# Reordered first loads and first squares, and a final norm's root taken with tokens on partitions, in a 2-layer decoder step on one core

## The chip, the cores and the metric

The kernel runs on one core of a Trainium2 chip, in one launch. The metric is the time of one execution on the device in microseconds (us), as the median of three runs. A profiled execution gives the trace from which the rows below are taken; its own time stands beside its span.

## What is computed

320 tokens (256 of a prompt, 64 of eight samples) of 1024 channels go through two layers, each a half-step SwiGLU, a mixer with three branches, and a second half-step SwiGLU, with an RMSNorm ahead of each and one at the end:

```python
def rmsnorm(x, g):
    y = xf * lax.rsqrt(jnp.mean(xf * xf, axis=-1, keepdims=True) + EPS)
    return y * g
for l in range(DEPTH):                       # DEPTH = 2
    x = x + 0.5 * swiglu_ffn(rmsnorm(x, ffn1_norm), w_gu, w_down)
    h = rmsnorm(x, mix_norm);  [u | v | q | g] = h @ w_in
    x = x + merged(pool(u), conv(v), attention(q), g) @ w_out
    x = x + 0.5 * swiglu_ffn(rmsnorm(x, ffn2_norm), w_gu2, w_down2)
y = rmsnorm(x, final_norm)
```

The change touches the very first RMSNorm and the loads ahead of it, the last RMSNorm, and the place at which a small state of the pooling branch is loaded.

## The kernel before

**Layout.** Channels lie on the 128 partitions: `x` is 128 x 8 x 320, eight blocks of 128 channels with the 320 tokens along the free dimension. A channel mean is therefore a matmul with a 128x128 matrix `ones` of value 1/1024, whose result stands on all partitions.

**Matmuls.** A product in full precision is made of three matmuls of split operands: the weight's high part times the activation's high and low parts (lines 306 and 307), then the weight's low part times the activation's high part (line 309). `chain` does this for 8 blocks at a time: 16 matmuls with `whi`, then 8 with `wlo`. These 24 matmuls use one half (128x1024) of a 1 MB weight tile `raw`; such a half is called a **unit** here and counted from 1.

**Weights.** `Stream` loads `raw` tiles through the queue of SyncE (SP), four in flight (`NRAW`), and `split` makes `whi` on ScalarE (ACT, a cast) and `wlo` on VectorE (DVE, a subtraction). There are four buffers each (`NW`), so the split of unit 9 writes the buffers of unit 5 and has to wait until TensorE (PE) has read them.

**The first SwiGLU.** The activations `hhi`, `hlo` are `x` times the norm's gain, split (`split_scaled`: ACT, then DVE, line 358 for ACT). They are not yet divided by the root of the mean square; that factor, `rstd`, is multiplied in when a result leaves PSUM (`sg<-mm,rstd`, `up<-mm,rstd`), since it depends only on the token. Products of units 1, 2, 3, 4, 5 go to PSUM buffers mm, mm, mm, cv, cv (`pwide`; three mm and two cv); unit 6 takes the mm buffer of unit 1 again, which is free when `sg<-mm,rstd` of unit 1 has read it.

**The factor.** `rsqrt_ops` is a chain of ten dependent DVE operations (`rx`) on 128x320, the last of which writes `rstd`. Ahead of it `first_mean` squares the eight blocks of `x` on GpSimd (POOL) and adds them up with eight matmuls on `ones` (line 901).

**The end.** The last mean is two matmuls on `ones` (lines 948 and 949: the sum of seven blocks' squares, and the eighth's square `last`), then `rsqrt_now` on 128x320, then `x` times `rstd`: blocks 6 and 7 on POOL, blocks 0 to 5 on DVE in three operations of 128x640, and the stores.

**Order.** The order of each engine's instructions is made when the program is built, by a scheduler that moves them; the order that came out is shown with the change. Operations on DVE and POOL are issued through a helper and all have line 124.

Of the kernel before, what the change touches and what calls it, by code (L numbers as in the profile page):

```python
# [15 lines left out]
P = 128  # L16
# [68 lines left out]
def trunk_kernel(  # L85
# [67 lines left out]
    def pst():  # L153
        return psum("st", 2)
# [3 lines left out]
    nc.scalar.dma_start(cst[:, :8], c_in[:, :8])  # L158
# [14 lines left out]
    class Stream:  # L173
# [11 lines left out]
        def issue(self):  # L185
            while self.pos < len(items) and self.live < NRAW:
# [10 lines left out]
                if it == ("w", 0):  # L197
                    for i in range(4):
                        if i < 2:
                            nc.sync.dma_start(t[:, 512 * i:512 * i + 512], src[:, 512 * i:512 * i + 512])  # L200
                        nc.sync.dma_start(x[:, 2 * i:2 * i + 2, :], x_in[:, 2 * i:2 * i + 2, :])
                    nc.sync.dma_start(t[:, 1024:], src[:, 1024:])
                    nc.gpsimd.dma_start(cst[:, 8:], c_in[:, 8:])
                else:
                    nc.sync.dma_start(t[:, :], src)
# [216 lines left out]
    def deferred_norm(l, off, squares=True):  # L422
# [4 lines left out]
        def on_block(o):  # L427
            split_scaled(x[:, o, :], ccol(l, off, o), h[0][:, o, :], h[1][:, o, :])
            if squares:
                st.add(x[:, o, :])  # L430
# [252 lines left out]
    def mixer(l, mh, acc, on_block):  # L683
# [81 lines left out]
        for g in range(4):  # L765
            ut = tp.tile([P, 2, UW], F32, name=nm("ut"), tag="ut", bufs=2)
            pool.memset(ut[:, :, 0:PB], 0.0)
            nc.gpsimd.dma_start(ut[:, :, PB + T:UW], sp_in[l, :, 2 * g:2 * g + 2, :])
# [120 lines left out]
    h, st, on_block = deferred_norm(0, C_G1, squares=False)  # L889
    for o in range(KB):  # L890
        if o % 4 == 1:
            ws.split(ws.nsplit)
            ws.nsplit += 1
        on_block(o)

    def first_mean():
        m = pst()
        for o in range(KB):
            s = t320("sq")
            pool.tensor_tensor(out=s[:, :], in0=x[:, o, :], in1=x[:, o, :], op=ALU.mult)  # L900
            nc.tensor.matmul(m[:, :T], ones[:, :], s[:, :], start=(o == 0), stop=(o == KB - 1))
        return m[:, :T]
# [45 lines left out]
    nc.tensor.matmul(m[:, :T], ones[:, :], fst.acc[:, :], start=True, stop=False)  # L948
    nc.tensor.matmul(m[:, :T], ones[:, :], last[:, :], start=False, stop=True)
    rsqrt_now(m[:, :T], T, rstd[:, :])  # L950
    for o in (6, 7):
        pool.tensor_tensor(out=x[:, o, :], in0=x[:, o, :], in1=rstd[:, :], op=ALU.mult)
    rb = rstd[:, :].rearrange("p (o t) -> p o t", o=1).to_broadcast([P, 2, T])
    for o in (0, 2, 4):
        dve.tensor_tensor(out=x[:, o:o + 2, :], in0=x[:, o:o + 2, :], in1=rb, op=ALU.mult)
        nc.sync.dma_start(y_out[:, o:o + 2, :], x[:, o:o + 2, :])
# [105 lines left out]
```

## Time and profile before

| | |
|---|---|
| median of three runs | 1659.54 us (1659.35 to 1659.97) |
| the profiled execution | 1659.87 us, span 1657.9 us, 1.97 us around it |
| TensorE busy | 1630.5 us, 98% of the span |
| first matmul starts | 5.83 us |
| last matmul ends | 1644.75 us |
| DVE busy | 1120.4 us, 68% of the span |

Times in rows count from the span's start. In a row of the timeline stand the start, the length from the first instruction's start to the last one's end, engine, line, operation, destination and source tiles, shapes, and how many instructions were merged; in brackets, how long the engine was idle before and on what it waited.

### The profile page before, as it was taken

The numbers are of one execution on the slowest core, as the hardware profiler recorded it, in microseconds if no ns is written. First come the engines' busy times: TensorE is split into PE (matmuls) and PEld (weight loads), VectorE is DVE, ScalarE is ACT, GpSimd is POOL, SyncE is SP. The second block draws the span as 40 slices with busy tenths as digits, with TensorE's granted clock in tenths as the row PEclk, the third lists the DMA queues.
The fourth block names the chain that finished last, engine by engine and source line by source line (L and its number), as shares of the span: only waits on it lengthen the run. The fifth ranks groups of instructions, "written<-read, shape, count | busy, mean of one in ns | idle before, by whom it ended". The sixth has DMA issues, their size and how long they took to land.

```text
span 1657.9 us, 27271 instructions
## 1 busy us (share of the span) xinstructions
PE 1630.5 (98%) x11194; PEld 1585.8 (96%) x11194; DVE 1120.4 (68%) x1854; ACT 784.0 (47%) x1167; POOL 266.7 (16%) x292
## 2 busy tenths in 40 slices
PE   8999999999999999999999999999999999999996
PEld 7999999998889999999999999999988899999996
DVE  7555647999975675554565564579998757655543
ACT  5444534456665444443344443354566544444341
POOL 2000001677520000000000000046674000000000
PEclk9999999999999999999999999999999999999998
DMA  7444446978976444444444444577798754444430
GB/s 276 153 151 145 169 169 199 266 231 238 294 260 229 151 155 151 144 146 149 149 153 153 153 153 166 189 220 232 235 278 254 267 199 153 145 145 147 150 126 32
DMA packets 47325, 305.73 MB, mean 184 GB/s; under 512 B 5728, under 2 KB 5792, under 8 KB 14048
## 3 DMA queue, kind: packets, MB, share of 16 engines
q1 hardware_dynamic: 38160, 270.75, 45.4%
q0 software_dynamic: 8752, 32.90, 9.2%
q8 instruction: 88, 1.44, 0.3%
q10 hardware_dynamic: 288, 0.33, 0.1%
q14 instruction: 37, 0.30, 0.0%
HBM read 295.14 MB, written 8.82 MB: 183 GB/s over the span
## 4 chain that ended last, share of the span: by engine, by line
PE 86%; DVE 7%; issue 3%; DMA 3%; ACT 1%; POOL 0%; DVEq 0%; SPq 0%; ACTq 0%; POOLq 0%
PE mm L306 19%; PE mm L309 19%; PE mm L307 19%; PE cv L309 8%; PE cv L306 8%; PE cv L307 8%; DVE cv L124 3%; DMA raw<-in_kc 2%; DVE us L124 1%; DVE wlo L124 1%; PE sa L665 1%; PE mm L484 1%; PE mm L483 1%; PE mm L487 1%; PE st L837 1%
## 5 line engine op out<-in xcount | busy, mean ns | idle before, releaser
L124 DVE TENSOR_TENSOR wlo<-raw,whi 128x1024 fp32r<-128x1024 f32 (+1 forms) x403 | 498.6, 1238 | 196.2 <-PE mm L309 85.7
L232 ACT CAST whi<-raw 128x1024 fp32r<-128x1024 f32 (+1 forms) x403 | 420.6, 1045 | 428.3 <-PE mm L307 252.9
L306 PE MATMUL mm<-hhi,whi 128*128 128x320 f32 x1712 | 512.3, 313 | 7.6 <-ACT hhi L358 5.8
L307 PE MATMUL mm<-hlo,whi 128*128 128x320 f32 x1712 | 507.8, 310 | 0.0
L306 PEld LDWEIGHTS mm<-hhi,whi 128*128 128x128 f32 x1712 | 321.6, 188 | 16.2 <-ACT hhi L358 6.6
L307 PEld LDWEIGHTS mm<-hlo,whi 128*128 128x128 f32 x1712 | 321.8, 188 | 1.9 <-DVE hlo L124 0.6
L309 PE MATMUL mm<-hhi,wlo 128*128 128x320 f32 x1712 | 289.4, 310 | 1.7 <-DMA wlo<-in_w 1.7
L309 PEld LDWEIGHTS mm<-hhi,wlo 128*128 128x128 f32 x1712 | 260.4, 188 | 2.7 <-DMA wlo<-in_w 2.2
L124 DVE SCALAR_TENSOR_TENSOR cv<-z,cst,cv 128x256 f32<-128x256 f32 x464 | 194.6, 476 | 0.2
L307 PE MATMUL cv<-hlo,whi 128*128 128x320 f32 x592 | 175.0, 310 | 0.0
L306 PE MATMUL cv<-hhi,whi 128*128 128x320 f32 x592 | 173.9, 309 | 0.0
L124 POOL MEMSET z<- 128x120 f32 x4 | 0.8, 196 | 820.5 <-PE mm L307 820.5
L124 POOL TENSOR_TENSOR pr<-pr 128x512 f32<-128x512 f32 (+3 forms) x128 | 122.7, 959 | 7.2
L306 PE MATMUL mm<-hidh,whi 128*128 128x320 f32 x418 | 123.9, 309 | 0.0
L307 PE MATMUL mm<-hidl,whi 128*128 128x320 f32 x418 | 123.7, 309 | 0.0
L362 ACT CAST hidh<-up 128x320 fp32r<-128x320 f32 x88 | 40.0, 459 | 159.8 <-DVE up L124 159.8
L307 PEld LDWEIGHTS cv<-hlo,whi 128*128 128x128 f32 x592 | 111.0, 188 | 0.2
L306 PEld LDWEIGHTS cv<-hhi,whi 128*128 128x128 f32 x592 | 110.8, 188 | 0.0
L309 PE MATMUL cv<-hhi,wlo 128*128 128x320 f32 x592 | 98.8, 309 | 0.0
L309 PEld LDWEIGHTS cv<-hhi,wlo 128*128 128x128 f32 x592 | 89.9, 188 | 0.2
L124 DVE TENSOR_TENSOR up<-mm,rstd 128x320 f32<-128x320 f32 x53 | 26.0, 490 | 87.8 <-PE mm L309 87.8
L306 PE MATMUL cv<-hidh,whi 128*128 128x320 f32 x286 | 84.7, 309 | 0.0
(196 smaller groups left out, 2336.2 us busy)
## 6 DMA issues: line engine op xcount, KB each, us to landing
raw<-in_w SPq DMA_DIRECT2D x221, 1024.0 KB, 4.8
wlo<-in_w POOLq DMA_DIRECT2D x42, 512.0 KB, 7.1
raw<-in_kc SPq DMA_DIRECT2D x16, 1024.0 KB, 7.3
raw<-in_vc SPq DMA_DIRECT2D x16, 1024.0 KB, 6.0
out_co<-z POOLq DMA_DIRECT2D x16, 135.0 KB, 6.4
raw<-in_mem SPq DMA_DIRECT2D x2, 1024.0 KB, 4.8
out_mk<-kt POOLq DMA_DIRECT2D x2, 1024.0 KB, 5.1
out_mv<-va POOLq DMA_DIRECT2D x2, 1024.0 KB, 9.5
```

The costliest lines, as they stand in the source:

```text
L124: return op(*args, **kw)
L232: nc.scalar.copy(h, r)
L306: nc.tensor.matmul(out, hi, xh, start=(i + e == 0), stop=False)
L307: nc.tensor.matmul(out, hi, xl, start=False, stop=False)
L309: nc.tensor.matmul(out, lo, xh, start=False, stop=(i + e == last))
L362: nc.scalar.copy(hi, src)
L483: nc.tensor.matmul(pv[mb][:, :], mh[0][:, k, mb * P:mb * P + P], wh, start=(k == 0), stop=False)
L484: nc.tensor.matmul(pv[mb][:, :], mh[1][:, k, mb * P:mb * P + P], wh, start=False, stop=False)
L487: nc.tensor.matmul(pv[mb][:, :], mh[0][:, k, mb * P:mb * P + P], wl, start=False, stop=(k == KB - 1))
L665: nc.tensor.matmul(po[32 * h:32 * h + 32, :256], pp[:, at:at + 32], raw[:, mb * 1024 + h * 256:mb * 1024 + h * 256 + 256], start=(bb == 0 ...
L837: nc.tensor.matmul(pv[:, :TP], vt[:, mb, o * P:o * P + P], kt[:, 2 * hd + mb, :], start=(mb == 0), stop=(mb == 1))
```

## The change

**Head.** The loads of the first weight tile's halves and of `x` are spread over two queues: SP's and ACT's. The gain of the first norm comes in a tile of its own, `g1`. The large table of constants `cst` (816 columns) is loaded after the first mean instead of at the start, and the first two loads of the pooling state `ut` wait for the layer's `q`. The first norm's squares move from POOL to ACT (two operations of 128x1280), are added on DVE, and need one matmul on `ones` in place of eight. `gate0` is a copy that holds the squares back until unit 2 has been split.

**Tail.** The last mean is taken with the tokens on partitions: three matmuls with 128 tokens each as stationary operand and one column of `ones`, for each of the two sources, give 128x3. The ten operations of the root run on 128x3. Three matmuls with the identity bring the factor back as 128x320 in PSUM (`fr`); ACT copies it to `rstd` for POOL, DVE multiplies with `fr` itself, and POOL's operations come after DVE's in the code.

```diff
-    nc.scalar.dma_start(cst[:, :8], c_in[:, :8])
+    g1 = tp.tile([P, 1280], F32, name="g1", tag="pr", bufs=1)
+    nc.scalar.dma_start(g1[:, :8], c_in[:, :8])
...
                 if it == ("w", 0):
-                    for i in range(4):
-                        if i < 2:
-                            nc.sync.dma_start(t[:, 512 * i:512 * i + 512], src[:, 512 * i:512 * i + 512])
-                        nc.sync.dma_start(x[:, 2 * i:2 * i + 2, :], x_in[:, 2 * i:2 * i + 2, :])
-                    nc.sync.dma_start(t[:, 1024:], src[:, 1024:])
-                    nc.gpsimd.dma_start(cst[:, 8:], c_in[:, 8:])
+                    nc.sync.dma_start(t[:, 0:512], src[:, 0:512])
+                    nc.scalar.dma_start(x[:, 0:2, :], x_in[:, 0:2, :])
+                    nc.sync.dma_start(t[:, 512:1024], src[:, 512:1024])
+                    nc.scalar.dma_start(x[:, 2:4, :], x_in[:, 2:4, :])
+                    nc.sync.dma_start(x[:, 6:8, :], x_in[:, 6:8, :])
+                    nc.scalar.dma_start(x[:, 4:6, :], x_in[:, 4:6, :])
+                    nc.scalar.dma_start(t[:, 1024:], src[:, 1024:])
...
             pool.memset(ut[:, :, 0:PB], 0.0)
+            dve.tensor_copy(ut[:, 0, PB + T:PB + T + 1], q[:, 0, 0:1])
             nc.gpsimd.dma_start(ut[:, :, PB + T:UW], sp_in[l, :, 2 * g:2 * g + 2, :])
...
-    h, st, on_block = deferred_norm(0, C_G1, squares=False)
+    h = new_h()
     for o in range(KB):
-        if o % 4 == 1:
-            ws.split(ws.nsplit)
-            ws.nsplit += 1
-        on_block(o)
+        if o == 1:
+            ws.split(0)
+        split_scaled(x[:, o, :], g1[:, o:o + 1], h[0][:, o, :], h[1][:, o, :])
+
+    ws.split(1)
+    ws.nsplit = 2
+    gate0 = tp.tile([P, 1280], F32, name="gate0", tag="pr", bufs=1)
+    dve.tensor_copy(gate0[:, 0:1], ws.units[1][1][:, 0:1].bitcast(F32))
 
     def first_mean():
-        m = pst()
-        for o in range(KB):
-            s = t320("sq")
-            pool.tensor_tensor(out=s[:, :], in0=x[:, o, :], in1=x[:, o, :], op=ALU.mult)
-            nc.tensor.matmul(m[:, :T], ones[:, :], s[:, :], start=(o == 0), stop=(o == KB - 1))
-        return m[:, :T]
+        acc = tp.tile([P, T], F32, name="acc0", tag="acc", bufs=1)
+        for i in range(2):
+            sq = tp.tile([P, 1280], F32, name=nm("sq4"), tag="pr", bufs=1)
+            nc.scalar.activation(sq[:, :].rearrange("p (k t) -> p k t", k=4), x[:, 4 * i:4 * i + 4, :], AF.Square)
+            dve.tensor_tensor(out=sq[:, :2 * T], in0=sq[:, :2 * T], in1=sq[:, 2 * T:], op=ALU.add)
+            if i == 1:
+                dve.tensor_tensor(out=acc[:, :], in0=acc[:, :], in1=sq[:, :T], op=ALU.add)
+            dve.tensor_tensor(out=acc[:, :], in0=acc[:, :] if i else sq[:, :T], in1=sq[:, T:2 * T], op=ALU.add)
+        dve.tensor_copy(cst[:, 8:9], acc[:, 0:1])
+        nc.gpsimd.dma_start(cst[:, 8:], c_in[:, 8:])
+        return mean_bc(acc[:, :], T)
...
-    nc.tensor.matmul(m[:, :T], ones[:, :], fst.acc[:, :], start=True, stop=False)
-    nc.tensor.matmul(m[:, :T], ones[:, :], last[:, :], start=False, stop=True)
-    rsqrt_now(m[:, :T], T, rstd[:, :])
-    for o in (6, 7):
-        pool.tensor_tensor(out=x[:, o, :], in0=x[:, o, :], in1=rstd[:, :], op=ALU.mult)
-    rb = rstd[:, :].rearrange("p (o t) -> p o t", o=1).to_broadcast([P, 2, T])
+    sm3 = t320("sm3")
+    cut = [(0, P), (P, P), (T - P, P)]
+    for src in (fst.acc, last):
+        for i, (c, n) in enumerate(cut):
+            nc.tensor.matmul(m[:n, i:i + 1], src[:, c:c + n], ones[:, 0:1], start=(src is fst.acc and i == 0),
+                             stop=(src is last and i == 2))
+    three = lambda i: sm3[:, 3 * i:3 * i + 3]
+    rsqrt3 = three(4)
+    for _ in rsqrt_ops(m[:, :3], 3, rsqrt3, [three(i) for i in range(4)]):
+        pass
+    fr = pst()[:, :T]
+    for i, (c, n) in enumerate(cut):
+        nc.tensor.matmul(fr[:, c:c + n], rsqrt3[:n, i:i + 1].to_broadcast([n, P]), ident[:n, :n],
+                         start=True, stop=True)
+    nc.scalar.copy(rstd[:, :], fr)
+    rb = fr.rearrange("p (o t) -> p o t", o=1).to_broadcast([P, 2, T])
     for o in (0, 2, 4):
         dve.tensor_tensor(out=x[:, o:o + 2, :], in0=x[:, o:o + 2, :], in1=rb, op=ALU.mult)
         nc.sync.dma_start(y_out[:, o:o + 2, :], x[:, o:o + 2, :])
+    for o in (6, 7):
+        pool.tensor_tensor(out=x[:, o, :], in0=x[:, o, :], in1=rstd[:, :], op=ALU.mult)
     nc.scalar.dma_start(y_out[:, 6:8, :], x[:, 6:8, :])
```

Three places of the built order follow. Numbers behind a tile's name tell buffers apart; in brackets are the engines or DMA queues whose semaphores an instruction waits for. In the changed kernel's rows, lines lie two higher than in the profile (306 is 308, 309 is 311).

VectorE, around the ten `rx` operations of the first root. Before, with the splits of units 5, 6 and 7 (`wlo_41`, `wlo_45`, `wlo_50`) between them, and the first result taken out of PSUM (`sg_25`) behind:

```order
L124 TENSOR_TENSOR wlo_41_211<-raw_3_93,whi_40_210 128x1024 [waits DMAHW1_49,Activation_49]
L124 TENSOR_TENSOR rx_38_198<-rx_37_197,rx_36_196 128x320 [waits DVE_49,Pool_49]
L124 TENSOR_TENSOR wlo_45_247<-raw_3_93,whi_44_246 128x1024 [waits PE_49,Activation_49]
L124 TENSOR_TENSOR rx_38_198<-rx_38_198,rx_37_197 128x320 [waits DVE_49]
L124 TENSOR_SCALAR rx_39_199<-rx_38_198 128x320 [waits DVE_49,Pool_49]
L124 TENSOR_TENSOR rx_39_199<-rx_39_199,rx_38_198 128x320 [waits DVE_49]
L124 SCALAR_TENSOR_TENSOR rx_37_197<-rx_39_199,rx_37_197 128x320 [waits DVE_49]
L124 TENSOR_TENSOR wlo_50_281<-raw_4_95,whi_49_280 128x1024 [waits DMAHW2_49,PE_49,Activation_49]
L124 TENSOR_TENSOR rx_38_198<-rx_37_197,rx_36_196 128x320 [waits DVE_49]
L124 SCALAR_TENSOR_TENSOR rx_38_198<-rx_38_198,rx_37_197 128x320 [waits DVE_49]
L124 SCALAR_TENSOR_TENSOR rstd_81<-rx_38_198,rx_37_197 128x320 [waits DVE_49]
L124 TENSOR_TENSOR sg_25_169<-mm_19_134,rstd_81 128x320 [waits DVE_49,Pool_49]
```

Now, where `wlo_52` is the split of unit 9 and `sg_24` takes unit 1's result out of PSUM:

```order
L124 TENSOR_TENSOR wlo_52_339<-raw_11_125,whi_51_338 128x1024 [waits DMAHW3_49,PE_49,Activation_49]
L124 TENSOR_SCALAR rx_29_186<-st_28_184 128x320 [waits PE_49]
L124 TENSOR_SCALAR rx_30_187<-rx_29_186 128x320 [waits DVE_49]
L124 TENSOR_TENSOR rx_31_188<-rx_30_187,rx_29_186 128x320 [waits DVE_49]
L124 TENSOR_TENSOR rx_31_188<-rx_31_188,rx_30_187 128x320 [waits DVE_49]
L124 TENSOR_SCALAR rx_32_189<-rx_31_188 128x320 [waits DVE_49]
L124 TENSOR_TENSOR rx_32_189<-rx_32_189,rx_31_188 128x320 [waits DVE_49]
L124 SCALAR_TENSOR_TENSOR rx_30_187<-rx_32_189,rx_30_187 128x320 [waits DVE_49]
L124 TENSOR_TENSOR rx_31_188<-rx_30_187,rx_29_186 128x320 [waits DVE_49]
L124 SCALAR_TENSOR_TENSOR rx_31_188<-rx_31_188,rx_30_187 128x320 [waits DVE_49]
L124 SCALAR_TENSOR_TENSOR rstd_82<-rx_31_188,rx_30_187 128x320 [waits DVE_49]
L124 TENSOR_TENSOR sg_24_170<-mm_18_135,rstd_82 128x320 [waits DVE_49]
```

The root's ten operations moved from between the splits of units 4 to 7 to behind the split of unit 9, with nothing in between.

TensorE, around the first mean's matmul. Before, the last of eight (line 901) stands between unit 1's matmuls with `wlo_9` and unit 2's first:

```order
L307 MATMUL mm_19_134<-hlo_6_98,whi_8_102 128x320 [waits DVE_49]
L309 MATMUL mm_19_134<-hhi_5_97,wlo_9_103 128x320 x8
L901 MATMUL st_27_171<-sq_35_193,ones_76 128x320 [waits Pool_49]
L306 MATMUL mm_26_170<-hhi_5_97,whi_10_116 128x320 [waits Activation_49]
L307 MATMUL mm_26_170<-hlo_6_98,whi_10_116 128x320
```

Now the only one (`st_28`, line 356) stands between unit 5's matmuls with `wlo_34` and unit 6's first, `mm_50`:

```order
L309 MATMUL cv_45_301<-hlo_6_98,whi_33_200 128x320
L311 MATMUL cv_45_301<-hhi_5_97,wlo_34_201 128x320 [waits DVE_49]
L311 MATMUL cv_45_301<-hhi_5_97,wlo_34_201 128x320 x7
L356 MATMUL st_28_184<-acc0_172,ones_77 128x320 [waits DVE_49,Pool_49]
L308 MATMUL mm_50_335<-hhi_5_97,whi_37_236 128x320 [waits DVE_49,Activation_49]
L309 MATMUL mm_50_335<-hlo_6_98,whi_37_236 128x320
```

The mean moved from behind unit 1 to behind unit 5, the last unit for which a PSUM buffer is free without an eviction; and unit 6's first matmul now waits for VectorE.

ScalarE, at the program's start. Before:

```order
L158 DMA cst_73<-in_cst 128x8
L232 ACT_TABLE_LOAD
L232 CAST whi_8_102<-raw_1_82 128x512 [waits DMAHW1_49]
L358 ACTIVATE hhi_5_97<-x_74,cst_73 128x320 [waits DMAHW2_49,DMAHW0_49]
L358 ACTIVATE hhi_5_97<-x_74,cst_73 128x320
L232 CAST whi_8_102<-raw_1_82 128x512 [waits DMAHW3_49]
```

Now, where DMAHW1 is the first half tile's own load and DMAHW3 the load of the first two blocks of `x`:

```order
L159 DMA g1_75<-in_cst 128x8
L200 DMA x_74<-in_x 128x640
L202 DMA x_74<-in_x 128x640
L204 DMA x_74<-in_x 128x640
L205 DMA raw_1_83<-in_w 128x1024 [waits DMAHW1_49]
L360 ACT_TABLE_LOAD [waits DMAHW3_49]
L360 ACTIVATE hhi_5_97<-x_74,g1_75 128x320 [waits DMAHW0_49]
L234 CAST whi_7_101<-raw_1_83 128x512
```

The table load moved from ahead of every wait to behind the arrival of `x`, and four more DMA issues stand in front of ScalarE's first work.

## Rows read from the trace of the kernel before

**Rows 1.** The page's first part: busy time of TensorE, share, instructions.

```profile
PE 1630.5 (98%) x11194; PEld 1585.8 (96%) x11194; DVE 1120.4 (68%) x1854; ACT 784.0 (47%) x1167; POOL 266.7 (16%) x292
```

**Rows 2.** TensorE's waits, whole span: total us, times, longest.

```profile
PE mm L306 <- ACT hhi L358: 5.8, 1, 5.8
...
PE mm L309 <- DMA wlo<-in_w: 2.3, 3, 1.4
```

**Rows 3.** Chain of waits, 0 to 60 us: start, length, engine, line.

```profile
1.19 3.94 DMA x<-in_x
5.21 0.57 ACT hhi L358
5.83 0.63 PE mm L306
...
9.64 0.27 PE mm L306
...
10.97 0.18 PE mm L307
...
14.90 1.17 PE mm L309 x8
...
29.52 1.17 PE cv L309 x8
...
33.04 1.17 PE mm L309 x8
```

**Rows 4.** Timeline of the head, 0 to 29 us, ScalarE and VectorE.

```profile
1.18 1.28 ACT L232 ACT_TABLE_LOAD   x1 [1.18 <-PEq L1035]
...
4.37 0.62 ACT L232 CAST whi<-raw 128x512 fp32r<-128x512 f32 x1 [1.90 <-DMA raw<-in_w]
...
7.87 0.69 DVE L124 TENSOR_TENSOR wlo<-raw,whi 128x512 fp32r<-128x512 f32 x1 [0.30 <-ACT whi L232]
...
8.66 2.89 ACT L358 ACTIVATE hhi<-x,cst 128x320 fp32r<-128x320 f32 x6 [0.82 <-DMA x<-in_x]
...
17.77 0.48 DVE L124 TENSOR_SCALAR rx<-st 128x320 f32<-128x320 f32 x1
...
26.53 0.49 DVE L124 TENSOR_TENSOR sg<-mm,rstd 128x320 f32<-128x320 f32 x1
...
28.14 1.22 DVE L124 TENSOR_TENSOR wlo<-raw,whi 128x1024 fp32r<-128x1024 f32 x1
```

**Rows 5.** Timeline of the tail, 1643 to 1653 us.

```profile
1643.41 0.47 ACT L943 ACTIVATE sq<-x 128x320 f32<-128x320 f32 x1 [8.61 <-DVE x L124]
...
1643.93 0.81 PE L949 MATMUL st<-sq,ones 128*128 128x320 f32 x2 [0.55 <-ACT sq L943]
1644.77 0.49 DVE L124 TENSOR_SCALAR rx<-st 128x320 f32<-128x320 f32 x1 [1.40 <-PE st L949]
...
1649.71 3.62 DVE L124 TENSOR_TENSOR x<-x,rstd 128x640 f32<-128x640 f32 x3
1649.82 2.82 POOL L124 TENSOR_TENSOR x<-x,rstd 128x320 f32<-128x320 f32 x2 [368.29 <-DVE rstd L124]
```

**Rows 6.** A half microsecond of the tail by stages; TensorE's granted clock is third last.

```profile
1649.00:1649.50 0.50, 0.00 (x0) 0.00 (x0) 0.47 (x2) 0.00 (x0) 0.00 (x0) 0.81 0.00 0
```

**Rows 7.** Line 124, VectorE: nanoseconds min/median/max, first and last start, shapes.

```profile
L124 DVE SCALAR_TENSOR_TENSOR cv<-z,cst,cv x464: 460/476/491, 284.5 to 1264.7; 128x256 f32<-128x256 f32 x155
...
L124 DVE SCALAR_TENSOR_TENSOR hlo<-x,cst,hhi x32: 540/547/1009, 5.8 to 1411.6; 128x320 fp32r<-128x320 f32 x32
```

**Rows 8.** Tile sm, VectorE: the kernel's smallest operations there.

```profile
L124 DVE RECIPROCAL sm<-sm x12: 146/150/167, 386.4 to 1282.3; 128x2 f32<-128x2 f32 x8, 128x1 f32<-128x1 f32 x4
```

**Rows 9.** Tile ut, ScalarE's copy out of PSUM.

```profile
L773 ACT COPY ut<-mm x16: 408/422/435, 386.3 to 1263.6; 128x320 f32<-128x320 f32 x16
```

**Rows 10.** Line 462: two fp32 passes of TensorE with 128 columns.

```profile
L462 PE MATMUL st<-cst,rmem x2: 271/272/272, 208.1 to 208.2; 128*128 128x128 f32 x2
```

More of the change, by code (lines that the diff above doesn't have):

```diff
@@ L420, in ffn, with deferred_norm @@
             on_block(o)
-    def deferred_norm(l, off, squares=True):
+    def deferred_norm(l, off):
         h = new_h()
@@ L428, in on_block @@
             split_scaled(x[:, o, :], ccol(l, off, o), h[0][:, o, :], h[1][:, o, :])
-            if squares:
-                st.add(x[:, o, :])
+            st.add(x[:, o, :])
         return h, st, on_block
```

## The prediction

> **What bounds the kernel now.** I read the busy times first, then what TensorE waits for, then the head and the tail as stretches of their own. TensorE is busy for 98% of the span [rows 1], so outside its gaps nothing but its own work counts. The longest of its gaps is the first, 5.8 us until the activations of the first SwiGLU exist [rows 2]; the loads of weights that GpSimd makes in the mixers cost it 2.3 us in all. The chain of waits in the head runs from the arrival of `x` (1.19 + 3.94 = 5.13 us) over ScalarE's first `hhi` to TensorE at 5.83 us, and stays on TensorE from there: unit 5 ends at 29.52 + 1.17 = 30.69 us, and unit 6 follows without a gap and ends at 33.04 + 1.17 = 34.21 us. A unit is thus 3.52 us of TensorE [rows 3]. The reader should also see there that a matmul takes 0.27 us at 9.64 us and that the faster ones begin at 10.97 us: TensorE ran at half its clock (1.2 GHz) for the first 5.1 us of its work. The root starts at 17.77 us and unit 1 leaves PSUM at 26.53 us, 4.2 us before unit 6 needs that buffer, so the root costs nothing now [rows 4]. In the tail everything is in series: square, mean, ten operations from 1644.77 to 1649.71 us (4.94 us), and the three multiplies, which end at 1653.33 us [rows 5].
>
> **Head, the start of unit 1.** ScalarE now issues four loads more, and its table load (1.28 us), which lay under the wait for data [rows 4], comes behind the arrival of `x`. I leave that arrival at 5.13 us [rows 3], since the same bytes but one more half weight tile share the way. ScalarE then needs 1.28 for the table, 0.57 for the first `hhi` and 2 x 0.62 for the first two casts, which is 8.2 us; the other seven `hhi` at 2.89 / 6 = 0.48 us end at 11.6 us [rows 3, 4]. VectorE makes the first `hlo` (0.55 us [rows 7]), two halves of `wlo` (0.69 each [rows 4]) and the second `hlo` by 7.0 + 0.55 + 1.38 + 0.55 = 9.5 us. At half clock a pair of matmuls takes 0.54 us, so TensorE sets the pace of the remaining pairs: 9.5 + 0.27 + 6 x 0.54 = 13.0 us. The eight matmuls with `wlo` take 1.17 us at full clock and twice that at half, so unit 1 ends between 14.2 and 15.2 us; I take 14.7. Before, it ended at 14.90 + 1.17 = 16.07 us, with one more pass of the mean behind it [rows 3]. So far the change is ahead by over a microsecond: the seven removed means and GpSimd's squares are gone.
>
> **Head, units 2 to 5.** Their weights are issued early, so they follow at 3.52 us each: unit 5 ends at 14.7 + 14.1 = 28.8 us, 1.9 us earlier than the 30.69 of now. The squares on ScalarE and their sums on VectorE lie under these units and cost nothing, as long as they are done by 28.8 us.
>
> **Head, the new wait.** Here the built order decides. The ten operations stand on VectorE behind the split of unit 9, which writes the buffer that unit 5 is read from; so it can't start before unit 5 ends. It takes 1.22 us, the ten operations take 4.94 us as in the tail, and the eviction of unit 1 takes 0.49 us [rows 4, 5]: 6.65 us, none of which can lie beside TensorE's work, because unit 6 needs the buffer that this eviction frees. Only the mean's matmul (0.81 us, the row of line 949 [rows 5]) runs under it. Unit 6 starts at 28.8 + 6.65 = 35.45 us in place of 30.69: **4.75 us later**. Queued behind unit 6 is all of TensorE's work, so this reaches the end in full.
>
> **Head, the clock.** TensorE is idle for 6.65 - 0.81 = 5.8 us. In the tail its last matmul ended at 1643.93 + 0.81 = 1644.74 us, and a mean of 0.81 over 1649.0 to 1649.5 us says that the grant fell from full to half at 1649.31 us, 4.6 us later [rows 6]. So the clock should fall before unit 6 starts. If it comes back as in the head, after 5.1 us of work, 5.1 us at 0.27 us a matmul do what needs 1.17 / 8 = 0.146 each at full clock: a loss of 5.1 x (1 - 0.146 / 0.27) = **2.35 us**, and nothing if the clock doesn't fall.
>
> **Middle.** The constants are first read at the end of the first SwiGLU, 44 units later; the `ut` loads now wait for the first of eight `q` products, seven products (24.6 us) before their reader. Both cost nothing. Two more issues stand on GpSimd's queue ahead of a weight load, which is asked for three units (10.6 us) early; without that cover the price would add to the 2.3 us of [rows 2], under 1 us.
>
> **Tail.** The square ends at 1643.41 + 0.47 = 1643.88 us [rows 5]. Behind it come three matmuls with one column each, two passes each. Their price isn't shown: from below half of the present 0.81 us, from above 1.4 us (six passes at 0.19 and the present drain of 0.27); I take 1.15 with the start, nearer the upper, since each pass loads its own 128x128. The ten operations on three columns are nearest to `sm`'s, 0.15 us [rows 8], with 0.03 between: 1.9 us, 3.0 less. Three matmuls with the identity, two passes each, start about 0.14 apart and end 0.27 behind the last [rows 10]: 1.05 us. ScalarE's copy takes 0.42 us [rows 9], 0.45 with its start, and VectorE waits for it too. The multiplies then start at 1643.88 + 1.15 + 1.9 + 1.05 + 0.45 = 1648.43 us, 1.3 earlier than now. Three operations of 640 columns would take 3 x 0.82 (0.49 for 320 and 1.22 for 1024 columns give 0.82), but take 3.62 us now, while GpSimd runs beside them [rows 4, 5]. With the factor in PSUM, VectorE has one operand in SBUF. The `cv` operations of the mixers, which have one as well and run beside GpSimd, spread only from 460 to 491 ns, while `hlo` with two goes from 540 to 1009 [rows 7]. So I take 2.46 us, and for GpSimd its present 2.82 as the upper end: both done between 1650.9 and 1651.25 us instead of 1653.33. **2.3 us gained**; bounds 0.8 (3.62 us, and the upper prices of the matmuls) and 3.0.
>
> The Trainium skill, GPSIMD Engine Reference, Specifications, says that GpSimd's SBUF interfaces are shared with VectorE and collide with its instructions that have two SBUF inputs. By it the multiplies with a factor in PSUM would run free of GpSimd, as the rows of `cv` and `hlo` have it; by the 3.62 us of now the tail would gain 1.2 us instead of 2.3.
>
> The Trainium skill, ScalarE: Activation LUTs, What ACT_TABLE_LOAD costs, states a drain of about 1.38 us beside the load, 2.66 us in all, which speaks against the table load's new place. By it unit 1 would end up to 1.4 us later and the sum would be 1.4 us worse; the trace has 1.28 us for the load, and no run here shows what a drain adds in this place.
>
> **Sum**, against the profiled execution's 1659.87 us: +4.75 + 2.35 - 2.3 = +4.8, which gives 1664.67. The median lies 0.33 below that execution, so 1664.3 us. Its own range: unit 1's end +-0.5, the clock 1.6 to 2.4, the tail -0.8 to -3.0, or 1662.4 to 1666.3.
>
> **The rivals.**
> - **The clock holds.** The fall in the tail came after 4.6 us, the new idle time is 5.8; that is not far apart, and it is one row only. Then the 2.35 us fall away: 1661.95, not slower by what can be told. It decides this if TensorE's first matmuls of unit 6 take 0.146 us.
> - **The loads collide.** Two queues and a third weight tile issued earlier share the engines that move data, so `x` and the second half of the first tile come later; one half tile's worth is about 0.7 us, two queues against each other up to 2. Against it: the 0.66 MB or so of constants and `ut` are out of the way. Time: 1665.0 to 1666.3.
> - **The root stays hidden.** If VectorE got through the split of unit 9 and the root before TensorE runs out of buffers, unit 6 would start after unit 5 and the mean, at 28.8 + 0.8 = 29.6, 1.1 us earlier than now, and with the tail the time is 1659.54 - 1.1 - 2.3 = 1656.1: faster. It needs the split not to wait for unit 5. Against it stand the order of both engines and four buffers.
>
> **Chances.** Forecast 0.62, clock holds 0.18, loads collide 0.12, root hidden 0.08. About 0.2% (3.3 us) is what a measurement of this kernel can tell from no change. Faster by more: 0.08, the last rival. Within: 0.15 of the second case and the low end of the forecast, 0.07, in all 0.22. Slower: 0.70. The range that holds 8 in 10 goes from 1661.2 to 1666.8.
>
> **What would show it.** Right: one wait of TensorE of about 6 us ahead of unit 6, for VectorE's `sg`, with the ten `rx` running back to back in it after a `wlo` that itself waited for TensorE; unit 1's end near 14.7 us; matmuls of 0.27 us at unit 6's start; `sm3` operations of 0.15 us and x multiplies of about 0.8 us in the tail. Wrong: no such wait, or `rx` starting well before unit 5 ends; a wait of unit 2 for its weights; multiplies of 1.2 us or more.

## The result, and the profile after

The changed kernel takes 1669.84 us (median of 4 runs, 1667.66 to 1671.25); the kernel before took 1659.68 us beside it (1659.35 to 1659.97). The ratio is 1.006, with a 95% interval of 1.0043 to 1.0078: 10.2 us slower, where 4.8 were forecast. The profiled execution took 1667.66 us, its span is 1665.8 us.

TensorE's waits over the whole span (total us, times, longest), against [rows 2]:

```profile
PE mm L308 <- ACT whi L234: 8.6, 1, 8.6
PE mm L308 <- DVE sg L124: 6.3, 1, 6.3
PE mm L311 <- DMA wlo<-in_w: 4.8, 4, 2.8
```

Three things are new. The first matmul waits 8.6 us instead of 5.8; there is a wait of 6.3 us for VectorE's `sg`, the one forecast; and the waits for the weights that GpSimd loads in the mixers have doubled (2.3 before). Where does the late first unit come from? The timeline of ScalarE in the head, with its DMA issues (`ACTq`), answers to [rows 4]:

```profile
2.15 0.45 ACTq L204 DMA_DIRECT2D x<-in_x  x1
4.32 0.34 ACTq L205 DMA_DIRECT2D raw<-in_w  x1
6.21 1.28 ACT L360 ACT_TABLE_LOAD   x1 [6.21 <-DMA x<-in_x]
7.50 0.56 ACT L360 ACTIVATE hhi<-x,g 128x320 fp32r<-128x320 f32 x1
...
13.15 1.02 ACT L360 ACTIVATE hhi<-x,g 128x320 fp32r<-128x320 f32 x2 [1.78 <-DMA x<-in_x]
16.91 3.90 ACT L234 CAST whi<-raw 128x1024 fp32r<-128x1024 f32 x4 [2.74 <-DMA raw<-in_w]
```

The first piece of `x` is in at 6.1 us (5.13 before) with the table load behind it, so the first matmul starts at 8.62. The last piece was issued at 2.15 us and is in at 13.1; the second half of the first weight tile, issued at 4.32, is in at 16.9. ScalarE stands still for both. The view of the DMA queues from 5 to 10 us (packets, MB, share of the engines that move data; q1 is SyncE's queue, q10 ScalarE's) says why:

```profile
q1 hardware_dynamic: 288, 1.49, 71.6%
q10 hardware_dynamic: 274, 0.64, 32.3%
```

The two queues send almost the same number of packets, but ScalarE's are rows of 2.5 KB of `x`, while SyncE's, once its own piece of `x` is in at 7.17 us, are rows of 8 KB of the 1 MB tiles, which nobody needs yet. So ScalarE's queue, which has only `x` to load here, gets 0.64 MB of 2.13; from 8 to 13 us it is 0.60 MB against 1.52, with 208 packets each. The Trainium skill, DMA: Bandwidth & Descriptors, Queues, rings and completion order, says that each engine that moves data takes turns between queues packet by packet; the equal counts agree. From 13.2 to 16.8 us, when only the half tile is left on ScalarE's queue, the counts are 147 and 64, so equal turns are shown for the stretch of `x` alone.

The chain of waits from the late `x` to the start of unit 6 (start, length, engine, line; lines 308, 309 and 311 are the 306, 307 and 309 of before), against [rows 3]:

```profile
16.59 1.40 PE mm L311 x8
...
31.19 1.19 PE cv L311 x8
...
32.45 1.23 DVE wlo L124
...
38.52 0.50 DVE sg L124
...
39.16 0.60 PE mm L308
39.77 0.27 PE mm L309
...
43.77 1.45 PE mm L311 x8
```

Unit 1 ends at 17.99 us, unit 5 at 32.38. Then VectorE makes the split of unit 9, the ten operations and the eviction one after the other, and unit 6 starts 6.78 us after unit 5's end, on a matmul of 0.27 us. The clock by stages (third last column):

```profile
36.00:38.00 2.00, 0.00 (x0) 0.00 (x0) 1.86 (x5) 0.00 (x0) 0.00 (x0) 0.86 0.00 0
38.00:40.00 2.00, 0.84 (x3) 0.87 (x4) 1.97 (x5) 0.63 (x2) 0.00 (x0) 0.50 0.00 0
...
42.00:44.00 2.00, 2.00 (x9) 2.00 (x9) 0.42 (x2) 0.20 (x1) 0.00 (x0) 0.50 0.00 0
44.00:46.00 2.00, 2.00 (x15) 2.00 (x14) 0.75 (x2) 0.85 (x1) 0.00 (x0) 0.93 0.00 0
```

Unit 6 runs at half clock almost to its end, at 43.77 + 1.45 = 45.22 us. Before, it ended at 34.21 [rows 3]: **the head costs 11.0 us**. The tail, against [rows 5]:

```profile
1653.29 0.47 ACT L954 ACTIVATE sq<-x 128x320 f32<-128x320 f32 x1 [8.61 <-DVE x L124]
...
1653.82 0.83 PE L963 MATMUL st<-ones,sq 128*128 128x1 f32 x6 [0.52 <-ACT sq L954]
1654.68 0.16 DVE L124 TENSOR_SCALAR sm<-st 128x3 f32<-128x3 f32 x1 [1.42 <-PE st L963]
...
1656.69 1.65 PE L971 MATMUL st<-cst,sm 128*128 128x128 f32 x6 [2.05 <-DVE sm L124]
1658.38 0.42 ACT L973 COPY rstd<-st 128x320 f32<-128x320 f32 x1 [4.02 <-PE st L971]
1658.84 2.28 DVE L124 TENSOR_TENSOR x<-x,st 128x640 f32<-128x640 f32 x3 [2.20 <-ACT rstd L973]
1658.88 1.68 POOL L124 TENSOR_TENSOR x<-x,rstd 128x320 f32<-128x320 f32 x2 [368.44 <-ACT rstd L973]
```

From the end of the last square (1653.76) to the end of the span are 12.0 us, where there were 14.0 (1657.9 - 1643.88): **the tail gains 2.0 us**. The last square starts at 1653.29 instead of 1643.41, 9.9 us later, so between the two the profiled execution won back 1.1 us. There (60 to 1640 us) TensorE waited 6.4 us in all, against 7.7 in the kernel before: 2.5 more for `wlo`, but 2.6 less for the tiles `raw<-in_kc` and 2.1 less for ScalarE's copies `ut`. With 11.0 - 1.1 - 2.0 = 7.9 it is 7.8 us above that of before; but it was the fastest of its four, the median lies 2.2 us higher, and the runs spread over 3.6 us, where the four of before spread over 0.6. So the middle was an open question too.

### The profile page after: what moved, and what is told of

The parts are those of the page before. It is cut to its first block, busy times and chain, and to the rows that moved or that the text cites. A ratio compares the mean times of both kernels' runs of the same rounds, so it can differ in the third digit from the quotient of the medians.

```text
span 1665.8 us, 27283 instructions
## 1 busy us (share of the span) xinstructions
PE 1633.2 (98%) x11194; PEld 1588.6 (95%) x11194; DVE 1118.5 (67%) x1869; ACT 787.5 (47%) x1170; POOL 259.8 (16%) x284
## 4 chain that ended last, share of the span: by engine, by line
PE 87%; DVE 5%; DMA 3%; issue 2%; POOL 1%; ACT 1%; ACTq 0%; DVEq 0%; POOLq 0%
PE mm L308 20%; PE mm L311 20%; PE mm L309 19%; PE cv L308 8%; PE cv L309 8%; PE cv L311 8%; DMA wlo<-in_w 2%; DVE cv L124 2%; DVE wlo L124 1%; PE sa L666 1%; POOL pr L124 1%; DVE us L124 1%; PE st L839 1%; PE sa L641 1%; DMA x<-in_x 1%
```

## Experiments

My theory after this result: `x` and the half tile are late because ScalarE's queue runs beside the 1 MB tiles; the root adds its wait because it stands behind unit 9's split, and the clock falls in that wait; the tail is a plain gain. Rivals: other parts of the head (table load, constants, big tiles issued earlier) make unit 1 late; the wait only follows from the late loads. Each time is the median, with the ratio to the kernel before on the same chip. Every kernel computes the whole reference.

**The tail alone.** The kernel before with the new code behind the last FFN.

> The head and the middle of before, the tail of after. Theory (the tail gains on its own what its trace shows, 14.0 to 12.0 us from the last square's end to the end of the span): 1657.7 us, 2.0 under before, and the three multiplies at 0.82 us each with GpSimd's two at 0.86. Rival (part of that gain is the head's doing, or the profiled tail was a lucky one): between 1658.5 and 1659.7. The slowdown of after is then all in the head, +12.2 us by the theory.

Measured: 1657.79 us (11 runs, 1656.92 to 1659.14), ratio 0.9984, interval 0.9975 to 0.9993; three multiplies in 2.28 us, GpSimd's two in 1.68. As expected. The loss is all ahead of the tail.

**Two edits undone, each alone and together.** Loads of `x` and the first tile back on SyncE's queue:

```diff
-                    nc.sync.dma_start(t[:, 0:512], src[:, 0:512])
-                    nc.scalar.dma_start(x[:, 0:2, :], x_in[:, 0:2, :])
...
-                    nc.scalar.dma_start(t[:, 1024:], src[:, 1024:])
+                    for i in range(4):
+                        if i < 2:
+                            nc.sync.dma_start(t[:, 512 * i:512 * i + 512], src[:, 512 * i:512 * i + 512])
+                        nc.sync.dma_start(x[:, 2 * i:2 * i + 2, :], x_in[:, 2 * i:2 * i + 2, :])
+                    nc.sync.dma_start(t[:, 1024:], src[:, 1024:])
```

> As after, but x and the first weight tile come on SyncE's queue in the order of before; only the first norm's constants stay on ScalarE's. Theory (ScalarE's queue got a small share beside the 1 MB tiles of SyncE's, which made x and the second half of the first tile late): x is in by 5 to 7 us, unit 1 ends near 15 us instead of 18.0. The root's ten operations start before the split of unit 9 in this build, but that split still stands behind the sixth of them, so the wait ahead of unit 6 shrinks to 1.2 + 4 x 0.5 + 0.5 = about 4 us and does not vanish: unit 6 starts near 34 us, and the time is 1662 us, 1664 if the clock falls in this wait too. Rival (the constants' later load, the third weight tile issued earlier or the table load's place made unit 1 late, whatever the queue): unit 1 still ends after 17 us and the time stays above 1666.

GpSimd's squares and eight matmuls for the mean again:

```diff
-        acc = tp.tile([P, T], F32, name="acc0", tag="acc", bufs=1)
...
-        return mean_bc(acc[:, :], T)
+        m = pst()
+        for o in range(KB):
+            s = t320("sq")
+            pool.tensor_tensor(out=s[:, :], in0=x[:, o, :], in1=x[:, o, :], op=ALU.mult)
+            nc.tensor.matmul(m[:, :T], ones[:, :], s[:, :], start=(o == 0), stop=(o == KB - 1))
+        pool.tensor_copy(cst[:, 8:9], s[:, 0:1])
+        nc.gpsimd.dma_start(cst[:, 8:], c_in[:, 8:])
+        return m[:, :T]
```

> As after, but the first squares are GpSimd's and the first mean is eight matmuls, as before; the constants' load still waits for it. Theory: x is as late as in after (near 13 us) and unit 1 ends near 18 us, but the ten operations of the root lie between the splits ahead of unit 9's, so TensorE waits less than 1 us ahead of unit 6 and its clock stays at 1.0: unit 6 starts near 33.3 us instead of 39.05, and the time is 1669.8 - 5.7 - 2.4 = 1661.7, give or take 1 us. Rival (the wait only follows from the late loads, and GpSimd's slower squares move it, not remove it): unit 6 still starts after 37 us and the time stays above 1666.

> Both edits together: loads of the head in one queue and squares on GpSimd as before, the constants and the ut loads as in after, the tail of after. Theory: unit 6 starts within 1 us of the 30.69 of before and nothing waits ahead of it, so the tail's 2.0 us are kept: 1657.5, with 1656.5 if the later constants let unit 1 end earlier. Rival (the constants that load later or the ut loads that wait cost something in the middle): 1658.5 or more, above the kernel with the new tail alone.

With one queue: 1663.31 us (11 runs, 1660.9 to 1667.88), 1.0023 (1.0014 to 1.0032). Its chain of waits:

```profile
11.25 1.17 PE mm L309 x8
...
25.86 1.19 PE cv L309 x8
27.13 1.23 DVE wlo L124
...
31.90 0.60 PE mm L306
```

Unit 1 ends at 12.42 us instead of 17.99, 5.6 us earlier, and the wait of TensorE ahead of unit 6 is still there (4.9 us), with a matmul of 0.27 us behind it: two separate losses.

With the old mean: 1665.32 us (6 runs, 1660.54 to 1666.89), 1.0023 (1.0011 to 1.0036), 3.6 us over what was expected. `x` is as late as in the changed kernel (12.46 us), but unit 5's end at 32.41 + 1.17 = 33.58 is followed by unit 6 with no wait:

```profile
30.17 1.23 DVE L124 TENSOR_TENSOR wlo<-raw,whi 128x1024 fp32r<-128x1024 f32 x1 [0.49 <-PE cv L311]
...
32.43 0.49 DVE L124 TENSOR_TENSOR sg<-mm,rstd 128x320 f32<-128x320 f32 x1
```

The eviction is over before unit 5 is. So the second rival falls: the wait stays when the loads are early, and goes when they are late. Of the first only the constants fall, which load late with one queue too (at 22.7 us). The edit also put ScalarE's table load back to 1.18 us (6.21 in the changed kernel) and the first 1 MB tile's issue to 4.49 us (2.12), so the 5.6 us are not the queue's alone; the kernels with small rows and with held tiles, below, take them apart. The old mean's miss shows in the middle: its profiled execution (1665.1 us) ran twice at half clock, near 370 to 373 and 1189 to 1192 us, which costs about 1.7 us each time.

Both together: 1660.82 us (11 runs, 1657.94 to 1664.5), 1.0008 (0.9999 to 1.0017), although TensorE leaves the head no later than before (the eight matmuls that started at 43.60 us start at 43.56) and the new tail is in. This one missed by 3 us, and all three spread over 6 to 7 us; something in the middle costs. TensorE's waits in the profile of the last one (200 to 500 us), its clock there, and GpSimd's queue and the chain of waits ahead of it:

```profile
PE mm L309 <- DMA wlo<-in_w: 3.5, 3, 2.8
```

```profile
368.00:369.00 1.00, 0.80 (x5) 0.80 (x6) 1.00 (x4) 0.00 (x0) 1.00 (x1) 1.00 1.11 254
369.00:370.00 1.00, 1.00 (x6) 1.00 (x5) 1.00 (x4) 0.00 (x0) 0.76 (x1) 0.50 1.05 311
...
372.00:373.00 1.00, 1.00 (x7) 1.00 (x7) 0.00 (x0) 0.00 (x0) 1.00 (x2) 0.79 0.20 82
```

```profile
355.75 1.45 POOL L768 DMA_DIRECT2D ut<-in_sp  x2 [4.58 <-DVE ut L124]
357.19 0.95 POOL L227 DMA_DIRECT2D wlo<-in_w  x1
```

```profile
357.19 10.96 DMA wlo<-in_w
```

GpSimd stands 4.6 us at the `ut` loads, which now wait for a copy of `q`; the weight load behind them goes out at 357.2 us and lands at 368.15, and TensorE waits 2.8 us for it, until 368.20. Right behind this wait its clock falls to half for a good 3 us. The changed kernel's profiled execution has the same chain in the second layer, with a wait of 2.80 us that ends at 1192.40, and there the clock stays up:

```profile
1181.41 10.95 DMA wlo<-in_w
```

```profile
1193.00:1194.00 1.00, 1.00 (x9) 1.00 (x9) 1.00 (x4) 0.12 (x1) 0.98 (x1) 1.00 1.10 352
```

**The `ut` loads.** The changed kernel without the copy, and the kernel before with nothing but the copy:

```diff
             pool.memset(ut[:, :, 0:PB], 0.0)
+            dve.tensor_copy(ut[:, 0, PB + T:PB + T + 1], q[:, 0, 0:1])
             nc.gpsimd.dma_start(ut[:, :, PB + T:UW], sp_in[l, :, 2 * g:2 * g + 2, :])
```

> As after, without the copy of one element of q into ut, so GpSimd's ut loads again go out early. Theory (the loads that wait for q stand on GpSimd's queue ahead of the mixers' weight loads and delay them by a few us, differently in each run): the head keeps its 11 us of loss and the tail its 2 of gain, TensorE's waits for wlo in the mixers fall back to 2 to 3 us, the spread of the runs falls from 3.6 us to about 1, and the median is 1659.9 + 11 - 2 = 1668.9 against 1669.8. Rival (the spread and the wlo waits come with the head, as its loads arrive at other times): spread of 3 us or more and over 4 us of wlo waits.

> The kernel before with nothing but the copy of one element of q into ut, so only the ut loads move. Theory: TensorE's waits for wlo in the mixers rise from 2.3 us to 5 us or more, the runs spread over 3 us or more, and the median is 2 to 4 us above before, 1662 to 1664. Rival (as forecast, the cover of three units holds): within 1 us of before.

Without the copy: 1667.72 us (5 runs, 1667.35 to 1669.87), 1.0048 (1.0034 to 1.0062). It is lower than the changed kernel, but the intervals overlap, the waits for `wlo` are 3.9 us and not 2 to 3, and the runs spread over 2.5; alone it decides nothing. The copy alone: 1662.85 us (11 runs, 1658.79 to 1666.02), 1.0017 (1.0009 to 1.0026), so a copy of one element a partition costs 2.7 us and spreads the runs over 7, where 21 of before beside them spread over 1.8. Its profiled execution is the fastest of the eleven, and it shows the later load:

```profile
355.36 1.47 POOL L769 DMA_DIRECT2D ut<-in_sp  x2 [4.57 <-DVE ut L124]
356.82 0.95 POOL L227 DMA_DIRECT2D wlo<-in_w  x1
```

In the kernel before, the same load went out 3.1 us earlier:

```profile
353.74 0.89 POOL L227 DMA_DIRECT2D wlo<-in_w  x1 [3.16 <-ACT wlo L226]
```

That execution itself lost nothing. TensorE waited 4.4 us for `wlo` in it instead of 2.3 (5 or more were expected), but 6.6 us in all between 60 and 1640 us instead of 7.7, and it is 1.1 us faster than that of before. So the copy's price is shown by the eleven times; that it arises in the slower executions as in the trace above is argued.

Then the kernel with both undone, again without the copy:

> As the kernel with one queue and GpSimd's squares (1660.8), without the copy of q into ut. What is left of the change is the tail, the first constants apart and the rest of them later. Theory (the ut loads alone made that kernel 3 us slower than the tail alone): 1657.7, with a spread of at most 3 us, and no stretch of half clock between 20 and 1640 us. Rival (the later load of the constants takes part): above 1659.

Measured: 1657.28 us (11 runs, 1656.21 to 1658.84), 0.9981 (0.9972 to 0.9989). 3.5 us under the same kernel with the copy, a spread of 2.6, and between 100 and 1640 us the clock is 1.00:

```profile
100.00:1640.00 1540.00, 1532.94 (x10563) 1491.01 (x10562) 1047.03 (x1746) 737.62 (x1103) 254.03 (x272) 1.00 0.56 185
```

The two profiled executions differ by 3.5 us too (1661.37 and 1657.82). With the copy TensorE waited 9.1 us between 60 and 1640 us, without it 6.7, and the stretch at half clock cost about 1.7.

**What makes ScalarE's queue late.** Three edits of the changed kernel: SyncE's big tiles in pieces of 2 KB a row; the big tiles held back until `x` is in; only the half tile moved to SyncE's queue.

```diff
+                elif it[0] == "w" and self.pos < 4:
+                    for e in range(0, 2048, 512):
+                        nc.sync.dma_start(t[:, e:e + 512], src[:, e:e + 512])
```

> As after, but SyncE loads its three further 1 MB tiles of the head in pieces of 512 columns, 2 KB a row where they had 8 KB. Theory (ScalarE's queue was starved because the two queues take turns by rows or packets, and its rows of 2.5 and 4 KB moved less in a turn than 8 KB): x is in by about 7 to 8 us instead of 13.15, the second half of the first tile by about 10 instead of 16.9, and unit 1 ends near 15 us instead of 18.0. The order on VectorE changes with it (six of the ten operations stand ahead of unit 9's split), so the wait ahead of unit 6 shrinks to about 4.5 us: 1664 to 1666. Rival (SyncE's queue goes first whatever the size of its rows): x still after 11 us, unit 1's end after 17.

```diff
+                    if it[0] == "w" and 1 <= self.pos <= 3:
+                        nc.gpsimd.tensor_copy(t[:, 0:1], x[:, 5, 0:1])
+                        nc.gpsimd.tensor_copy(t[:, 1:2], x[:, 7, 0:1])
                     nc.sync.dma_start(t[:, :], src)
```

> As after, but SyncE's second to fourth weight tiles wait until x is in: GpSimd copies one element of each of the last two pieces of x into them first, and the load overwrites it. Theory (ScalarE's queue is late only because the 1 MB tiles run beside it): x is in by about 7 us instead of 13.15, the second half of the first tile by 8 to 9 instead of 16.9, and unit 1 ends at 14 to 15 us instead of 18.0; the tiles held come in time for unit 3. In this build six of the ten operations of the root stand ahead of unit 9's split, so the wait ahead of unit 6 is near 4 us and the time 1663 to 1666. Rival (loads that ScalarE issues are late by themselves, or two queues share evenly and the bytes decide): x still after 10 us.

```diff
-                    nc.scalar.dma_start(t[:, 1024:], src[:, 1024:])
+                    nc.sync.dma_start(t[:, 1024:], src[:, 1024:])
```

> As after, but the second half of the first weight tile is loaded by SyncE's queue, ahead of the 1 MB tiles; x stays on ScalarE's. Theory (x alone makes unit 1 late by about 2 us, and the half tile makes unit 2 late on top): x still near 11 to 13 us, the half tile in by about 8, unit 1 ends near 16.5 us and unit 2 follows it without a wait. Unit 9's split stands behind eight of the ten operations of the root, so the wait ahead of unit 6 is near 3.3 us: 1662 to 1665. Rival (with the half tile gone from it, ScalarE's queue brings x in by 9 us): unit 1 ends before 15.

With small rows the queues from 5 to 10 us read:

```profile
q10 hardware_dynamic: 371, 0.95, 50.4%
q1 hardware_dynamic: 379, 0.76, 43.4%
```

Equal packets again, and now ScalarE's queue has the larger part of the bytes. The last `x` is in at 2.15 + 8.1 = 10.3 us (later than the 7 to 8 expected, yet no `hhi` waits for it behind 8.84), the half tile at about 12.2, and unit 1 ends at 14.89 + 1.17 = 16.06. With the tiles held, `x` is in by 8.7 us and unit 2's cast starts at 12.17 with no wait for its half tile; unit 1 ends at 16.44, 1.4 us behind what was expected. No `hhi` waits for the last `x`, but the first one is still in at 6.1 us, with the table load behind it:

```profile
6.20 1.28 ACT L363 ACT_TABLE_LOAD   x1 [6.20 <-DMA x<-in_x]
...
15.10 1.34 PE mm L314 x8
```

With the half tile on SyncE's queue `x` is still late and the half tile is not, and unit 1 ends at 15.79 + 1.17 = 16.96:

```profile
9.96 1.05 ACT L234 CAST whi<-raw 128x1024 fp32r<-128x1024 f32 x1 [0.15 <-DMA raw<-in_w]
11.45 1.02 ACT L360 ACTIVATE hhi<-x,g 128x320 fp32r<-128x320 f32 x2 [0.43 <-DMA x<-in_x]
```

So it is the big rows beside it that bring the last `x` in at 13.1 us instead of 8.7 or 10.3, not the engine that issues. For unit 1's end they are worth 1.6 to 1.9 us (17.99 against 16.44 and 16.06). The other 3.6 to 4.0 us down to the 12.42 of one queue come with ScalarE's earlier start there (table load at 1.18 us, first matmul at 5.84 instead of 8.62); how they divide between the first `x` and the table load was not tested. The waits ahead of unit 6 were 4.0, 4.0 and 3.4 us, as the place of unit 9's split among the ten operations gave them. The times, 1667.35 (1.0044, 1.0031 to 1.0056), 1665.83 (1.0034, 1.002 to 1.0047) and 1664.49 us (1.002, 1.001 to 1.0029), carry the copy's spread and tell less than these rows; the first missed its range by 1.4 us, and its profiled execution has a stretch at half clock near 373 to 376 us.

**Two versions meant to be better.** Loads in one queue, `ut` as before, the new tail, and a cheaper mean that is not late. First GpSimd's squares summed on VectorE:

```diff
+            s = t320("sq")
+            pool.tensor_tensor(out=s[:, :], in0=x[:, o, :], in1=x[:, o, :], op=ALU.mult)
+            if o == 0:
+                prev = s
+            else:
+                dve.tensor_tensor(out=acc[:, :], in0=(prev if o == 1 else acc)[:, :], in1=s[:, :], op=ALU.add)
```

> A version meant to be better than both: loads of the head on SyncE's queue in the order of before, the constants later, GpSimd's squares summed on VectorE and one mean, the ut loads as before, the tail of after. In this build the root's ten operations stand ahead of the split of unit 9. Theory: no wait ahead of unit 6, unit 5 ends near 28.5 us instead of 30.69 (seven means fewer on TensorE), the clock holds, tail -2.0: 1655.5, between 1654.5 and 1656.5. Rival (VectorE, which now sums the squares between the hlo, is late with the last hlo, or the root is late again): 1657.5 or more.

Then pairs of squares added on GpSimd, and four matmuls:

```diff
+            if o % 2:
+                pool.tensor_tensor(out=s[:, :], in0=s[:, :], in1=sqs[-2][:, :], op=ALU.add)
+                nc.tensor.matmul(m[:, :T], ones[:, :], s[:, :], start=(o == 1), stop=(o == KB - 1))
```

> A version meant to be better than both: loads of the head on SyncE's queue in the order of before, the constants later, GpSimd squares and adds pairs of them (twelve operations near 1.0 us), four matmuls for the mean instead of eight, the ut loads as before, the tail of after. VectorE does nothing more than before among the hlo, and in this build the root's ten operations stand ahead of the split of unit 9. Theory: no wait ahead of unit 6, the clock is up by about 11 us, unit 5 ends 1 to 2 us earlier than 30.69, tail -2.0: 1656.5, between 1655.5 and 1657.3. Rival (TensorE, which takes its instructions in order, stands behind a mean whose pair is late): 1657.8 or more, no better than the tail alone.

Measured: 1661.05 us (11 runs, 1659.25 to 1665.49), 1.001 (1.0001 to 1.0019), and 1658.64 us (11 runs, 1657.44 to 1660.12), 0.9989 (0.998 to 0.9998). Both missed, with times as their rivals had them. No wait stands ahead of unit 6 in either, but VectorE is late with the `hlo`, on its timeline in the first and in the second:

```profile
9.30 1.93 DVE L124 SCALAR_TENSOR_TENSOR hlo<-x,g,hhi 128x320 fp32r<-128x320 f32 x2
11.15 1.00 DVE L124 TENSOR_TENSOR acc<-acc,sq 128x320 f32<-128x320 f32 x1
...
15.20 0.48 DVE L124 TENSOR_TENSOR acc<-acc,sq 128x320 f32<-128x320 f32 x1
```

```profile
8.50 5.93 DVE L124 SCALAR_TENSOR_TENSOR hlo<-x,g,hhi 128x320 fp32r<-128x320 f32 x6
```

Beside GpSimd's squares an addition takes 1.00 us, behind them 0.48; six `hlo` take 5.93 us, where the kernel with one queue and ScalarE's squares needs about 0.5 each. In the kernel before they reach 1.0 as well [rows 7], but its GpSimd is done with the squares at 14.1 us, and that of the second version at 18.7. Unit 1 ends at 19.66 us in the first and at 16.58 in the second, whose unit 5 ends at 32.28 and not 1 to 2 us ahead of 30.69. The first also spreads over 6 us without the copy. Its profiled execution (1662.79 us) has a wait of 2.1 us for `raw<-in_kc` at 455 us and half clock behind it until 459, so other waits than the copy's do this too; why here more often is open.

## Why the forecast was wrong, step by step

- **"I leave that arrival at 5.13 us".** This is the step that failed. In fact the first `x` came at 6.1 us, the last at 13.13 and the half tile at 16.9, just in time for unit 2, and unit 1 ended at 17.99 instead of 14.7: 3.3 us of the miss. The reason given, that the same bytes share the way, looks at the sum of bytes only; what counts is the share of one queue beside another. Of the 3.3 us, 1.6 to 1.9 go with the big rows (small rows, held tiles). The 1.4 to 1.7 us that stay without them are 0.9 to 1.1 for the first `x`, which came that much later on ScalarE's queue, and 0.4 to 0.7 in the pace of the first pairs, where TensorE waits for `hlo` twice; so the other numbers of this step were somewhat low as well (and 13.0 + 2.34 gives 15.3, not 15.2). The rival "the loads collide" named the cause but priced it at 0.7 to 2 us. A half tile alone, 512 KB, is 1.2 us at the 425 GB/s that both queues moved from 5 to 10 us, not 0.7, and the 2 us have no row behind them.
- **Units 2 to 5.** 14.4 us from unit 1's end to unit 5's, forecast 14.1.
- **The new wait.** Forecast 6.65 us, measured 6.78, with the split, the ten operations and `sg` in the order given. The kernel with the old mean shows that it goes when the root stands ahead of the split.
- **The clock.** Forecast 2.35 us; unit 6 took 45.22 - 39.16 = 6.06 us instead of 3.52, 2.5 more. It fell as argued from [rows 6], and the rival in which it holds did not come.
- **Middle: "Both cost nothing".** Failed for the `ut` loads. The step looked at who reads them, and gave the two issues behind a cover of three units; it left out that their waiting instruction holds GpSimd's queue for 4.6 us with a weight load behind it. Its bound was under 1 us; the copy alone costs 2.7 in the median. In the changed kernel it is 2.1 us by the medians with and without the copy (1669.84 and 1667.72, on different chips), less well known, since their intervals overlap. The later constants cost nothing that can be told: with them late the best kernel stands at 0.9981, and the tail alone at 0.9984.
- **Tail.** Forecast 2.3 us, measured 2.0. The six matmuls behind the square took 0.83 us and the ten operations 1.97, close to 1.15 and 1.9; the six with the identity took 1.65 instead of 1.05 (the granted clock is 0.50 there), and the multiplies 2.28 instead of 2.46. By the rule of the Trainium skill, GPSIMD Engine Reference, Specifications, the multiplies with a factor in PSUM run free of GpSimd, and the trace agrees: 0.82 us each, and GpSimd's own are 0.86 where they were 1.43. The drain that the Trainium skill, ScalarE: Activation LUTs, What ACT_TABLE_LOAD costs, states beside the load is not seen here: the load ran from 6.21 to 7.49 us and the next instruction started at 7.50.

In the profiled executions the head is +11.0 us, the middle -1.1 and the tail -2.0. By medians, head and tail together are +7.6 (the changed kernel without the copy, 1667.72 against 1660.12), the tail alone -2.1 (1657.79 against 1659.91), so the head about +9.7, and the copy the other 2 to 3; forecast were +7.1, 0 and -2.3. The best version is the old loads and the old mean with the new tail and the later constants, 1657.28 us; that its constants gain anything over the tail alone is within the intervals.

## What to carry to other kernels

When a small urgent load is moved to a second queue, look at the row sizes of what runs in the first: where two queues sent equal numbers of packets, the one with the bigger rows moved the bigger share (1.52 against 0.60 MB here), so the urgent load belongs ahead of the big one in the same queue, or the big one is held. An extra wait on an instruction is paid by whatever stands behind it in that engine's queue, so its price is read from the next issue on that queue, not from the reader of its data. And where a late split and a long chain of small operations share an engine, their order decides whether the chain is hidden.

## What the runs showed of the hardware that was not expected

- Two queues with work sent 208 packets each in 5 us (8 to 13 us), with a mean of 7.3 KB on one and 2.9 KB on the other; with rows of 2 KB on the first it was 379 and 371.
- A wait of TensorE of 2.82 us was followed by a good 3 us at half clock, and another of 2.80 us, behind the same chain, was not. Over all kernels, 13 waits of 1.9 to 2.8 us stand between 60 and 1640 us of the profiled executions; eight have such a stretch at their end or right behind, which costs about 1.7 us, and five do not. With the copy five of eight kernels show one or two, without it one of six.
- In the kernel with both edits undone but the copy left in, the mean clock of the eleven runs goes with their time, from 0.997 at 1657.94 us to 0.994 at 1664.5. As one stretch takes about 3 x 0.5 / 1660 = 0.001 off the mean, several such stretches in a run are my reading of the spread; only the profiled executions show them. The kernel before isn't free of slow executions either: of 28 beside the first four experiments, four took 1662.3 to 1665.1 us.
- GpSimd's squares double VectorE's additions of two SBUF operands, 0.48 to 1.00 us.
